# Turning scaled tiles by a product with a diagonal, and two moves in the order of a block's products

## The chip, the cores and the metric

The kernel runs on one core of one Trainium2 chip. The metric is the device time of one execution in microseconds (us), as the median of several runs. Engines are named as in the profile: PE (TensorE matmul) with PEld (its weight load), DVE (VectorE), ACT (ScalarE), POOL (GpSimd), SP (SyncE, whose queue issues the DMAs).

## The reference

One layer of a hybrid encoder block on 2048 tokens of width 1024, in float32:

```python
xn = rms_norm(x, ln_mix_g)
proj = xn @ w_in
y = concat(mlstm_group(proj...), mla_group(proj...))      # mLSTM in both directions, attention
h = x + y @ w_out                                         # "out" stage
h = h + conv_gated_mlp(rms_norm(h, ln_ffn_g))             # w_up, 3-tap conv, silu gate, w_down
gate = sigmoid(rms_norm(h, ple_norm_g) @ w_ple_gate)      # "gate" stage
h = h + gate * rms_norm(p @ w_ple_proj, ple_post_g)
return rms_norm(h, final_g)
```

`rms_norm(x, g)` is `x * rsqrt(mean(x*x) + 1e-6) * g` over the 1024 columns.

## The kernel before, in words

The tokens are cut into 16 tiles of 128 rows. After the input projection, the mLSTM and the attention, everything from `w_out` on runs in one loop, `Block.stream`, over "pairs" `i`: -8 to -1 is the out stage (two token tiles each), 0 to 43 the up projection of the MLP (two blocks of 22, one for each half of the tokens), 44 to 67 the down projection (three blocks of 8), 68 (`NG`) to 75 the gate stage. A run of pairs that shares its large operand is a block, so the block changes at i = 0, 22, 44, 52, 60 and 68.

Each pair computes a 2x2 block product by Strassen's method in Winograd's form, with seven products. `prod(out, w, x)` (line 1435) issues one of them: 128x128 pieces of the pair's own operand as weights against 512 columns of the block's operand. Both are split into a high and a low part (fp32r), and three of the four combinations are multiplied, 12 matmuls for four k pieces, 9 where the block has three. The order in program text is A11 B11 (into PSUM tile x, "fx" in the trace), S1 T1 (z, "fz"), A22 T4 of the pair before (`rest_y(prev)`, into its y, weights "fwd"), S2 T2 (y, "fy"), A12 B21 (x), S4 B22 of the pair before (`rest_z(prev)`, z), S3 T3 (y). A22 T4 accumulates in the same bank y that S3 T3 left, so the addition on DVE that reads S3 T3 (line 1420, into uv, xt or fh) comes before it.

The block's operands B11, T1, T2, B21, T3, T4 and B22 come by DMA as raw tiles ("opr", a few places in rotation), and `load_op` splits them: a cast on ACT (line 120, or 128 with a gain), then a subtraction on DVE (line 123, or 129 with a gain), into "op". `load(then, name)` does this for the next block, in the last pair of the block before. A raw tile's place is loaded anew (`op_fill`) once it is split. `up_prep` prepares the pair's own operand for the next pair ("fw", "fwd"), with the same casts and subtractions.

In the out stage, `Out.done` stores a finished tile t to h1_d by DMA and squares it on ACT with row sums; POOL makes the inverse norm r, a column of one value for each token. `Out.scaled` (line 1706) then multiplies the 128x1024 tile by r in place on ACT, and `Out.turn` turns it, four 128x128 transpositions (line 1716, with the identity `b.ident` as moving operand) into one PSUM bank, which ACT copies out (line 1718, or 1721 with a gain for i < -4) for the store to x2_d. `Out.beside` places these steps beside the products of later pairs: `scaled` at sides 7 and 1, the four turns of a pair's two tiles at sides 1 to 4 two pairs later.

In the gate stage the pair's own operand is made from tiles of h2_d: `load_tile` loads them ("ha"), `Gate.turn` transposes them (line 1842) at sides 1, 2, 4 and 5 of the pair before they are used. In the first gate pair, i = `NG`, side 1 turns tile 2. Its place, w7, held the first output tile of pair NG-2 until that was complete and stored by `rest_z` (line 1463).

The order on each engine is not that of the text. A planner orders the instructions of each engine from their order in the text and its own estimates of when their inputs are there. `keep_in_program_order(ins)` pins an instruction behind the one that stands before it in the text on the same engine.

Of the kernel before, what the change touches and what calls it, by code (L numbers as in the profile page):

```python
# [13 lines left out]
AF = mybir.ActivationFunctionType  # L14
ALU = mybir.AluOpType
# [4 lines left out]
P = 128  # L20
# [15 lines left out]
SB = 512  # L36
# [24 lines left out]
class Block:  # L61
# [51 lines left out]
        t = self.smp.tile([P, 1 if n == 1 else 8], F32, name=name, tag="c1" if n == 1 else "c8")  # L113
        return t[:, 0:n]

    def split(self, src, hi, lo, act=True, sub=None):

        nc = self.nc
        if act:
            nc.scalar.copy(hi, src)  # L120
        else:
            nc.vector.tensor_copy(hi, src)
        (sub or nc.vector).tensor_tensor(lo, src, _f(hi), op=ALU.subtract)  # L123

    def split_g(self, src, g, hi, lo):

        nc = self.nc
        nc.scalar.activation(hi, src, AF.Copy, scale=g)
        nc.vector.scalar_tensor_tensor(lo, src, g, _f(hi), op0=ALU.mult, op1=ALU.subtract)

    def mm3(self, out, lh, ll, rh, rl, first, last, more=False):

# [1141 lines left out]

    def load_op(self, blk, n):

        self.xop[n] = [self.early.get((blk, n, k)) or self.split_op() for k in range(self.BLOCKS[blk][2])]

    def split_soon(self, n):

# [1 line left out]
            item = self.loaded[0][0]  # L1282
            self.early[item] = self.split_op()

    def split_op(self):

        (blk, n, k), raw, _ = self.loaded.pop(0)
        hi, lo = self.op_place(blk, n, k)
        gain = {2: self.g2, 6: self.g3}.get(blk)
        if gain is not None and n[0] == "B":  # L1290
            kt = k + (int(n[1]) - 1) * 4
            self.split_g(raw, gain[0][:, kt:kt + 1], hi, lo)
        else:
            self.split(raw, hi, lo)
        self.op_fill()
        return hi, lo

# [118 lines left out]
    def stream(self, out):  # L1416

        nc = self.nc
# [5 lines left out]
        first = self.o  # L1424
# [1 line left out]
        class Pair:  # L1426
            pass

        def prod(out, w, x, more=False, cols=slice(0, SB)):
            wh, wl = w  # L1430
            ops = self.xop[x]
            first, last = not more, len(ops) - 1
            for a, lo in ((wh, 0), (wl, 0), (wh, 1)):
                for k, parts in enumerate(ops):
                    nc.tensor.matmul(out, a[:, k * P:(k + 1) * P], parts[lo][:, cols], start=first,  # L1435
                                     stop=lo == 1 and k == last, skip_group_check=more)
                    first = False

        def rest_y(s):

            prod(s.y, s.ops["A22"], "T4", True)
            if s.acc:
                add(s.o[1][:, L], s.o[1][:, L], s.y)
                if s.out:
                    first.done(s, 1)
                    return
                nc.sync.dma_start(self.h2_d[2 * s.pr + 1], s.o[1])
                if s.i >= gate.first - 8:
                    gate.factor(s.o[1], 2 * s.pr + 1)
            elif s.gate:  # L1450
                gate.part(s, 1, 0, s.y)
            else:
                nc.scalar.copy(s.uv[:, 2:2 + SB], s.y)

        def rest_z(s):

            prod(s.z, s.ops["S4"], "B22", True)
            if s.acc:
                add(s.o[0][:, H], s.o[0][:, H], s.z)
                if s.out:  # L1460
                    first.done(s, 0)
                    return
                nc.sync.dma_start(self.h2_d[2 * s.pr], s.o[0])
                if s.i >= gate.first - 8:
                    gate.factor(s.o[0], 2 * s.pr)
            elif s.gate:
                add(s.c12, s.c12, s.z)
                gate.part(s, 0, 1, s.c12)
            else:
                add(s.ug[:, 2 + SB:2 + 2 * SB], s.ug[:, 2 + SB:2 + 2 * SB], s.z)  # L1470
# [42 lines left out]
        prev, n = None, blocks[-1][0] + blocks[-1][1]  # L1513
# [7 lines left out]
        NG = NUP + 24  # L1521
        for i in range(blocks[0][0], n):
            blk = max(q for q, bl in enumerate(blocks) if bl[0] <= i)
            j = i - blocks[blk][0]
            then = blk + 1 if j == blocks[blk][1] - 1 and blk + 1 < len(blocks) else None

            def load(b, name):
                if b is not None:
                    self.load_op(b, name)

            def side(at):

                bank = prev.spare if at % 2 and prev else s.spare
                first.beside(s, at, bank)
                gate.beside(s, at, bank)

            s = Pair()
# [6 lines left out]


            prod(x, s.ops["A11"], "B11")
            nc.scalar.copy(s.y, x)  # L1547
            if s.acc:
                s.o = first.tiles if s.out else outs.pop(i)
            load(then, "B11")  # L1550
            side(1)
            prod(s.z, s.ops["S1"], "T1")
            if not s.acc:
                s.p5 = self.at("t4" if s.gate else f"t{6 + i % 2}", [P, SB], name="p5")
                nc.scalar.copy(s.p5, s.z)
            load(then, "T1")
            side(2)
            if prev:
                rest_y(prev)
                if prev.up:  # L1560
                    conv(prev, 1)
            if i == n - 1:
                rest_z(prev)
            if j == 0 and blk:
                load(blk, "T4")
            side(3)
            prod(s.y, s.ops["S2"], "T2", True)
            if s.acc:
                add(s.o[0][:, H], s.o[0][:, H], s.y)
            elif s.gate:  # L1570
# [12 lines left out]
                self.up_prep(i + 1)  # L1583
            if 0 <= i < NG - 2:
                self.up_load(i + 2)
            prod(x, s.ops["A12"], "B21", True)
            if s.acc:
                add(s.o[0][:, L], s.o[0][:, L], x)
            elif s.gate:
# [4 lines left out]
            if NG <= i + 1 < n:  # L1594
                self.up_prep(i + 1)
            if prev and i < n - 1:
                rest_z(prev)
                if prev.up:
                    conv(prev, 0)
            if j == 0 and blk:  # L1600
# [3 lines left out]
            if NUP < i < NG - 1:  # L1604
                outs[i + 1] = self.down_out(i + 1)
            side(6)
            load(then, "B21")
            prod(s.y, s.ops["S3"], "T3", True)
            if i == NUP:
                c22 = self.at("t7", [P, SB], name="c22")  # L1610
                nc.scalar.copy(c22, s.y)
                add(c22, c22, s.z)
                s.o += self.down_out(NUP, (1,))
                add(s.o[1][:, H], s.o[1][:, H], c22)
                outs[i + 1] = self.down_out(i + 1)
            elif s.acc:
                add(s.o[1][:, H], s.o[1][:, H], s.y)
                add(s.o[1][:, H], s.o[1][:, H], s.z)
            elif s.gate:
                add(s.p5, s.p5, s.y)  # L1620
                gate.part(s, 1, 1, s.p5)
            else:
                s.uv = self.at("u2", [P, 2 * SB + 2], name="uv")
                add(s.uv[:, 2 + SB:2 + 2 * SB], s.p5, s.y)
                if i in steps:
                    self.p1tag = f"t{6 + i % 2}"
                    next(steps[i])
            load(then, "T3")
            side(7)
            if i < NG - 2 and any(bl[0] + bl[1] - 2 == i for bl in blocks[:-1]):  # L1630
                self.op_begin(blk + 1)
            prev = s
# [21 lines left out]
class Out:  # L1654
# [3 lines left out]
    def __init__(self, b):  # L1658
        self.b, self.nc, self.d = b, b.nc, b.d
        self.rot, self.tiles, self.next, self.norm = _rot("", ("w11", "u2", "u0", "u1", "w7")), None, [], {}  # L1660
        self.parts = {}

    def tile(self, i, e):

# [38 lines left out]

    def scaled(self, i, e):
        t, r = self.norm[i, e]
        self.nc.scalar.activation(t, t, AF.Copy, scale=r)

    def turn(self, i, e, f, bank):

        b, nc = self.b, self.nc  # L1710
        t, c = self.norm[i, e][0], self.tile(i, e)
        xo = b.at(f"t{4 + f if i > -5 else 2 * e + f}", [P, 4, P], name="nt_o")
        pt = bank.rearrange("p (k t) -> p k t", t=P)
        for j in range(4):
            kt = f * 4 + j
            nc.tensor.transpose(pt[:, j], t[:, kt * P:(kt + 1) * P], b.ident)
        if i > -5:
            nc.scalar.copy(xo, pt)
        else:
            for j in range(4):  # L1720
                nc.scalar.activation(xo[:, j], pt[:, j], AF.Copy, scale=b.g2[0][:, f * 4 + j:f * 4 + j + 1])
            self.parts[f, e] = xo
        nc.sync.dma_start(b.x2_d[:, f * 4:f * 4 + 4, c * P:(c + 1) * P], xo)
# [321 lines left out]
```

## Time and profile before

| | |
|---|---|
| median of 3 runs | 2899.16 us (2894.27 to 2899.87) |
| profiled execution | 2900.96 us, of which the span of the trace is 2899.2 |
| PE busy | 2853.5 us, 98% of the span |
| DVE, ACT, POOL busy | 2041.1, 1524.4, 158.0 us |
| DMA | 508.94 MB, mean 176 GB/s |
| out stage, in the trace | from about 1232 us; its last turn at 1435 us |
| change from block 1 to block 2 | about 1806 to 1840 us |
| first gate pair | begins at 2717.40 us |

A row of a group in the profile gives line, engine, operation, output and inputs, count, then busy us, mean ns of one, and the idle time of the engine before them with what ended it. A row of the timeline gives start, duration (of a merged run of instructions), engine, line, names, shape, count, and in brackets the idle time before it and its releaser. Matmuls are pipelined: the duration of one is longer than the distance to the next one's start.

### The profile page before, as it was taken

Reading aid. Unit: us, or ns where it says so; the run is one execution under the profiler, and the core shown is the slowest. Engines: PE = TensorE matmul, PEld = TensorE weight load, DVE = VectorE, ACT = ScalarE, POOL = GpSimd, SP = SyncE. Lnnn points to the kernel's source line nnn. Section 1 sums busy time; section 2 is a strip of 40 time slices with the busy share of each in tenths; the row PEclk is TensorE's granted clock in tenths of the full one; section 3 lists DMA queues with packets and bytes.
Section 4 is the critical chain, followed back from the end, with each engine's and each line's share of the span. In section 5 each row is a group of like instructions: output and inputs, shape, how many; then the busy total and the mean of one; then the engine's idle time right before and its main releaser. Section 6 shows DMA issues by size and latency. Waiting matters only on the chain.

```text
span 2899.2 us, 40167 instructions
## 1 busy us (share of the span) xinstructions
PE 2853.5 (98%) x14110; PEld 2390.1 (82%) x14110; DVE 2041.1 (70%) x3790; ACT 1524.4 (53%) x3014; POOL 158.0 (5%) x295
## 2 busy tenths in 40 slices
PE   8999999999999999999999999999999999999998
PEld 7888888888888888788788888788888788888787
DVE  7521555777777777876677877767777867576787
ACT  7311544556666566765755555655555423254765
POOL 3100000000000010001000000000000000002111
PEclk9999999999999999999999999999999999999999
DMA  6612545653333333478834554657776757476865
GB/s 194 127 59 76 162 122 165 218 160 118 107 111 97 97 116 110 129 240 266 266 139 170 188 178 141 212 179 232 231 240 207 243 176 263 158 260 213 274 214 163
DMA packets 408314, 508.94 MB, mean 176 GB/s; under 512 B 34080, under 2 KB 271664, under 8 KB 408112
## 3 DMA queue, kind: packets, MB, share of 16 engines
q1 hardware_dynamic: 408112, 506.37, 55.3%
q8 instruction: 111, 1.82, 0.3%
q14 instruction: 91, 0.75, 0.1%
HBM read 324.16 MB, written 182.12 MB: 175 GB/s over the span
## 4 chain that ended last, share of the span: by engine, by line
PE 84%; DMA 5%; DVE 5%; ACT 3%; issue 3%; POOL 1%; SPq 0%; ACTq 0%; POOLq 0%; DVEq 0%
PE fy L1435 21%; PE fz L1435 14%; PE fx L1435 14%; PE bk L133 13%; PE ppv L989 3%; PE tb L977 3%; PE bk L914 2%; PE bk L916 2%; PE bk L915 2%; PE bk L918 2%; PE bk L917 2%; PE fs L133 2%; PE ppv L990 2%; PE gb L133 1%; PE mb L852 1%
## 5 line engine op out<-in xcount | busy, mean ns | idle before, releaser
L1435 PE MATMUL fz<-op,fw 128*128 128x512 f32 x1968 | 477.1, 391 | 2.7 <-ACT fw L120 2.7
L1435 PE MATMUL fy<-op,fw 128*128 128x512 f32 x1968 | 478.1, 391 | 1.6 <-ACT fy L1547 1.6
L1435 PE MATMUL fx<-op,fw 128*128 128x512 f32 x1968 | 476.0, 390 | 0.0
L1435 PEld LDWEIGHTS fy<-op,fw 128*128 128x128 f32 x1968 | 370.4, 189 | 79.4 <-ACT fy L1547 2.4
L1435 PEld LDWEIGHTS fz<-op,fw 128*128 128x128 f32 x1968 | 367.5, 188 | 79.5 <-ACT fw L120 3.6
L1435 PEld LDWEIGHTS fx<-op,fw 128*128 128x128 f32 x1968 | 368.0, 188 | 76.2 <-ACT fy L1547 0.2
L1435 PE MATMUL fy<-op,fwd 128*128 128x512 f32 (+1 forms) x984 | 239.8, 392 | 2.8 <-DVE uv L1420 2.6
L120 ACT CAST pt<-tb 128x512 fp32r<-128x512 f32 x256 | 147.2, 587 | 171.2 <-PE tb L977 170.4
L133 PE MATMUL bk<-wsp,xh 128*128 128x512 f32 (+1 forms) x768 | 234.1, 386 | 0.0
L1435 PEld LDWEIGHTS fy<-op,fwd 128*128 128x128 f32 x984 | 183.7, 189 | 41.7 <-DVE uv L1420 3.7
L919 DVE TENSOR_REDUCE mx<-bk 128x1 f32<-128x512 f32 x256 | 174.7, 684 | 40.5 <-PE bk L918 39.3
L123 DVE TENSOR_TENSOR pt<-tb,pt 128x512 fp32r<-128x512 f32 x256 | 174.1, 684 | 30.7 <-ACT pt L120 28.9
L937 ACT ACTIVATE pe<-bk,nm 128x512 f32<-128x512 f32 x256 | 174.8, 696 | 38.2 <-DVE nm L931 33.5
L989 PE MATMUL ppv<-pt,kv 128*128 128x512 f32 x512 | 188.6, 406 | 0.5 <-DVE pt L123 0.5
L133 PEld LDWEIGHTS bk<-wsp,xh 128*128 128x128 f32 x768 | 145.2, 189 | 25.1
L133 PE MATMUL bk<-wsp,xl 128*128 128x512 f32 (+1 forms) x384 | 150.7, 392 | 7.7 <-DVE xl L123 7.7
L133 PE MATMUL bk<-xh,wqk 128*128 128x512 f32 x480 | 157.1, 393 | 0.0
L977 PE MATMUL tb<-ident,pe 128*128 128x128 f32 x1024 | 150.3, 273 | 4.4 <-DVE pt L123 3.8
L990 PE MATMUL ppv<-pt,kv 128*128 128x256 f32 x512 | 144.7, 283 | 0.0
L977 PEld LDWEIGHTS tb<-ident,pe 128*128 128x128 f32 x1024 | 121.8, 140 | 25.0 <-DVE pt L123 6.8
L120 ACT CAST fw<-hraw 128x1024 fp32r<-128x1024 f32 (+1 forms) x72 | 70.2, 980 | 116.4 <-PE fx L1435 58.9
L123 DVE TENSOR_TENSOR fw<-fwr,fw 128x1024 fp32r<-128x1024 f32 x88 | 107.4, 1220 | 26.9 <-ACT fw L120 26.9
(363 smaller groups left out, 5113.5 us busy)
## 6 DMA issues: line engine op xcount, KB each, us to landing
fwr<-in_w_up SPq DMA_DIRECT2D x66, 512.0 KB, 5.2
fh<-h_d SPq DMA_DIRECT2D x48, 512.0 KB, 4.2
h_d<-fh SPq DMA_DIRECT2D x48, 512.0 KB, 4.0
s_d<-fwr SPq DMA_DIRECT2D x44, 512.0 KB, 3.3
fws<-s_d SPq DMA_DIRECT2D x44, 512.0 KB, 3.7
rw<-row_d SPq DMA_DIRECT2D x32, 512.0 KB, 5.5
tw_d<-tsum SPq DMA_DIRECT2D x60, 256.0 KB, 5.4
opr<-tw_d SPq DMA_DIRECT2D x60, 256.0 KB, 4.7
```

What stands on the lines that cost most here:

```text
L120: nc.scalar.copy(hi, src)
L123: (sub or nc.vector).tensor_tensor(lo, src, _f(hi), op=ALU.subtract)
L133: mm = lambda *a, **k: self.nc.tensor.matmul(*a, **k, skip_group_check=more)
L914: mm(ps, ql, kh[:, ks], start=True, stop=False)
L915: mm(ps, qr, self.krl[:, ks], start=False, stop=False)
L916: mm(ps, qh, kl[:, ks], start=False, stop=False)
L919: nc.vector.tensor_reduce(s.mx[:, kb:kb + 1], ps, axis=AX.X, op=ALU.max)
L937: nc.scalar.activation(s.pe[:, kb % 2], s.banks[kb], AF.Exp, bias=s.nm, scale=ASCALE, accum_out=s.rs[:, kb:kb + 1])
L977: nc.tensor.transpose(t[:, j, :], s.p[kb][:, j * P:(j + 1) * P], self.ident)
L989: mm(w.ps, vh[:, ks], pts[kb][:, j], start=kt == 0, stop=False, skip_group_check=True)
L990: mm(w.ps[:, 0], vl[:, ks], pts[kb][:, j, 0], start=False, stop=kt == NT - 1, skip_group_check=True)
L1435: nc.tensor.matmul(out, a[:, k * P:(k + 1) * P], parts[lo][:, cols], start=first, stop=lo == 1 and k == last, skip_group_check=more)
```

## The change

Three edits.

1. `Out.scaled` no longer scales the tile. It writes a 128x128 tile "diag", the identity times r, in a place of its own (s0 or s1), and `Out.turn` replaces each transposition by an ordinary f32 product of the tile's 128x128 piece with that diagonal.
2. `load(then, "B21")` moves from ahead of S3 T3 to behind S3 T3's addition, ahead of `load(then, "T3")`; the DVE halves of these splits are pinned in the order of the text.
3. At i = NG, `rest_y(prev)` (A22 T4 of the last down pair) moves from behind side 2 to between side 1 and S1 T1. The first matmul of each of A22 T4, S1 T1, S2 T2, A12 B21 and S4 B22 of the pair before is pinned there in the order of the text.

```diff
-    def split(self, src, hi, lo, act=True, sub=None):
+    def split(self, src, hi, lo, act=True, sub=None, pin=False):
...
-        (sub or nc.vector).tensor_tensor(lo, src, _f(hi), op=ALU.subtract)
+        a = (sub or nc.vector).tensor_tensor(lo, src, _f(hi), op=ALU.subtract)
+        if pin:
+            self.tc.keep_in_program_order(a)
...
-        self.xop[n] = [self.early.get((blk, n, k)) or self.split_op() for k in range(self.BLOCKS[blk][2])]
+        self.xop[n] = [self.early.get((blk, n, k)) or self.split_op(n == "B21") for k in range(self.BLOCKS[blk][2])]
...
-                    nc.tensor.matmul(out, a[:, k * P:(k + 1) * P], parts[lo][:, cols], start=first,
-                                     stop=lo == 1 and k == last, skip_group_check=more)
-                    first = False
+                    m = nc.tensor.matmul(out, a[:, k * P:(k + 1) * P], parts[lo][:, cols], start=first,
+                                         stop=lo == 1 and k == last, skip_group_check=more)
+                    if pin:
+                        self.tc.keep_in_program_order(m)
+                    first = pin = False
...
             load(then, "B11")
             side(1)
-            prod(s.z, s.ops["S1"], "T1")
+            if i == NG:
+                rest_y(prev, True)
+            prod(s.z, s.ops["S1"], "T1", pin=i == NG)
...
             side(2)
-            if prev:
+            if prev and i != NG:
                 rest_y(prev)
...
-            prod(s.y, s.ops["S2"], "T2", True)
+            prod(s.y, s.ops["S2"], "T2", True, pin=i == NG)
...
-            prod(x, s.ops["A12"], "B21", True)
+            prod(x, s.ops["A12"], "B21", True, pin=i == NG)
...
-                rest_z(prev)
+                rest_z(prev, i == NG)
...
             side(6)
-            load(then, "B21")
             prod(s.y, s.ops["S3"], "T3", True)
...
+            load(then, "B21")
             load(then, "T3")
...
     def scaled(self, i, e):
         t, r = self.norm[i, e]
-        self.nc.scalar.activation(t, t, AF.Copy, scale=r)
+        dg = self.diag[i, e] = self.b.at(f"s{e}", [P, P], name="diag")
+        self.nc.scalar.activation(dg, self.b.ident, AF.Copy, scale=r)
...
-            nc.tensor.transpose(pt[:, j], t[:, kt * P:(kt + 1) * P], b.ident)
+            nc.tensor.matmul(pt[:, j], t[:, kt * P:(kt + 1) * P], self.diag[i, e], start=True, stop=True)
```

More of the change, by code (lines that the diff above doesn't have):

```diff
@@ L122, in split, with split_g @@
             nc.vector.tensor_copy(hi, src)
-        (sub or nc.vector).tensor_tensor(lo, src, _f(hi), op=ALU.subtract)
-    def split_g(self, src, g, hi, lo):
+        a = (sub or nc.vector).tensor_tensor(lo, src, _f(hi), op=ALU.subtract)
+        if pin:
+            self.tc.keep_in_program_order(a)
+    def split_g(self, src, g, hi, lo, pin=False):
         nc = self.nc
         nc.scalar.activation(hi, src, AF.Copy, scale=g)
-        nc.vector.scalar_tensor_tensor(lo, src, g, _f(hi), op0=ALU.mult, op1=ALU.subtract)
+        a = nc.vector.scalar_tensor_tensor(lo, src, g, _f(hi), op0=ALU.mult, op1=ALU.subtract)
+        if pin:
+            self.tc.keep_in_program_order(a)
     def mm3(self, out, lh, ll, rh, rl, first, last, more=False):
@@ L1283, in split_soon, with split_op @@
             self.early[item] = self.split_op()
-    def split_op(self):
+    def split_op(self, pin=False):
         (blk, n, k), raw, _ = self.loaded.pop(0)
@@ L1291, in split_op @@
             kt = k + (int(n[1]) - 1) * 4
-            self.split_g(raw, gain[0][:, kt:kt + 1], hi, lo)
+            self.split_g(raw, gain[0][:, kt:kt + 1], hi, lo, pin)
         else:
-            self.split(raw, hi, lo)
+            self.split(raw, hi, lo, pin=pin)
         self.op_fill()
@@ L1427, in stream, with prod @@
             pass
-        def prod(out, w, x, more=False, cols=slice(0, SB)):
+        def prod(out, w, x, more=False, cols=slice(0, SB), pin=False):
             wh, wl = w
@@ L1434, in prod, with rest_y @@
                 for k, parts in enumerate(ops):
-                    nc.tensor.matmul(out, a[:, k * P:(k + 1) * P], parts[lo][:, cols], start=first,
-                                     stop=lo == 1 and k == last, skip_group_check=more)
-                    first = False
-        def rest_y(s):
-            prod(s.y, s.ops["A22"], "T4", True)
+                    m = nc.tensor.matmul(out, a[:, k * P:(k + 1) * P], parts[lo][:, cols], start=first,
+                                         stop=lo == 1 and k == last, skip_group_check=more)
+                    if pin:
+                        self.tc.keep_in_program_order(m)
+                    first = pin = False
+        def rest_y(s, pin=False):
+            prod(s.y, s.ops["A22"], "T4", True, pin=pin)
             if s.acc:
@@ L1453, in rest_y, with rest_z @@
                 nc.scalar.copy(s.uv[:, 2:2 + SB], s.y)
-        def rest_z(s):
-            prod(s.z, s.ops["S4"], "B22", True)
+        def rest_z(s, pin=False):
+            prod(s.z, s.ops["S4"], "B22", True, pin=pin)
             if s.acc:
@@ L1660, in __init__ @@
         self.rot, self.tiles, self.next, self.norm = _rot("", ("w11", "u2", "u0", "u1", "w7")), None, [], {}
-        self.parts = {}
+        self.parts, self.diag = {}, {}
     def tile(self, i, e):
```

## The prediction

> **What bounds the kernel now.** I read the page's first part, then who PE waited for from 1236 us to the end (out stage to gate stage), then the stretches, then the timeline around each wait that is left.
>
> ```profile
> PE 2853.5 (98%) x14110; PEld 2390.1 (82%) x14110; DVE 2041.1 (70%) x3790; ACT 1524.4 (53%) x3014; POOL 158.0 (5%) x295
> ```
> ```profile
> PE fz L1435 <- ACT fw L120: 2.7, 2, 1.8
> PE fs L1716 <- ACT nt_o L1718: 2.7, 1, 2.7
> PE fy L1435 <- DVE uv L1420: 2.6, 2, 1.8
> PE fs L1716 <- ACT xt L1706: 2.0, 1, 2.0
> PE fy L1435 <- ACT fy L1547: 1.6, 1, 1.6
> PE fs L1842 <- DMA ha<-h_d: 0.9, 1, 0.9
> PE fy L1435 <- DVE xt L1420: 0.2, 1, 0.2
> ```
> ```profile
> 1250.00:1380.00 130.00, 130.00 (x619) 107.39 (x618) 86.04 (x118) 75.19 (x160) 15.88 (x36) 1.00 0.79 251
> 1380.00:1390.00 10.00, 7.30 (x31) 5.74 (x30) 6.94 (x12) 8.97 (x17) 0.00 (x0) 0.83 0.52 149
> ```
>
> The columns of the waits are total us, times, longest; those of a stretch its length, then PE, PEld, DVE, ACT and POOL busy, granted clock, DMA share and GB/s. PE is the bound. In 1663 us it waits 12.7 us, in nine places. From 1250 to 1380 us, the heart of the out stage, it has no gap at all: whatever a changed instruction adds to PE there is added to the end, and relief of ACT or DVE is worth only the waits in that list and the slower products behind them (granted clock 0.83 where a gap of 2.7 us falls).
>
> **The turns: what they cost on PE.** The change makes each transposition of line 1716 a plain f32 product with a scaled diagonal. A plain f32 product of 128x128 by 128 columns exists in this kernel: line 838, the mLSTM scores, called 4 times in each of 16 chunks.
>
> ```profile
> L838 PE MATMUL mb<-qk 128*128 128x128 f32 x128 | 17.2, 275 | 0.0
> ...
> L1716 PE MATMUL fs<-ident,xt 128*128 128x128 f32 x128 | 19.7, 278 | 4.7 <-ACT nt_o L1718 2.7 <-ACT xt L1706 2.0
> ```
> ```profile
> 735.66 1.05 PE L838 MATMUL mb<-qk 128*128 128x128 f32 x8
> 736.47 0.47 PE L914 MATMUL bk<-kv,q_s 128*128 128x512 f32 x1
> ...
> 1342.60 0.60 PE L1716 MATMUL fs<-ident,xt 128*128 128x128 f32 x4
> 1342.96 2.99 PE L1435 MATMUL fx<-op,fw 128*128 128x512 f32 x12
> ```
>
> Line 838 has 64 calls and 128 records, line 1716 has 128 calls (16 tiles of 8) and 128 records: a plain f32 product runs as two, a transposition as one. In time it is the same two to one: four products are eight records and hold PE from 735.66 to 736.47, 0.81 us; four transpositions from 1342.60 to 1342.96, 0.36 us. So a group of four grows by 0.45 us, and there are 32 groups (16 tiles, two halves): **+14.4 us**. No gap can hide it before 1380 us. The ends are 0, if the second record slipped under the stream of large products, and three times more, 1.08 us a group, if the array needed four of what a transposition needs. I take 0.45, since line 838's eight stand in just such a stream of 512-column products. By the Trainium skill ("TensorE: Matmul & The Clock Gate", Terms) its transpose mode is four times faster for FP32, and "FP8 and Floating Point Precision" (TensorE Precision Notes) gives true FP32 four passes; by these the term would be about +35 us, an estimate, and the trace of line 838 speaks for half of that ratio.
>
> **The turns: what they free on ACT.**
>
> ```profile
> L1706 ACT ACTIVATE xt<-xt,rsr 128x1024 f32<-128x1024 f32 x16 | 18.5, 1153 | 25.1 <-DMA h_d<-xt 23.4 <-issue 0.8 <-POOL rsr L143 0.8
> ```
> ```profile
> L862 ACT ACTIVATE hy<-mb,den 128x128 f32<-128x128 f32 x64 | 20.3, 371 | 12.0 <-DVE den L858 10.6 <-PE bk L917 1.4
> ```
> ```profile
> 1379.85 1.15 ACT L1706 ACTIVATE xt<-xt,rsr 128x1024 f32<-128x1024 f32 x1 [5.77 <-DMA h_d<-xt]
> ...
> 1428.98 1.15 ACT L1706 ACTIVATE xt<-xt,rsr 128x1024 f32<-128x1024 f32 x1 [0.69 <-DMA h_d<-xt]
> ```
> ```profile
> 1384.12 1.11 PE L1716 MATMUL fs<-ident,xt 128*128 128x128 f32 x4 [2.70 <-ACT nt_o L1718]
> 1384.89 4.11 PE L1435 MATMUL fy<-op,fw 128*128 128x512 f32 x12
> ...
> 1430.18 0.66 PE L1716 MATMUL fs<-ident,xt 128*128 128x128 f32 x4 [1.95 <-ACT xt L1706]
> 1430.59 4.58 PE L1435 MATMUL fy<-op,fw 128*128 128x512 f32 x12
> ```
>
> Line 1706 scales the tile in place, so it must wait until the store to h1_d has read it: 23.4 us of ACT standing still, with casts and copies queued behind. The new instruction writes 128x128 into a place of its own; line 862, a copy with a column's scale of that size, takes 0.371 us against 1.153. ACT gets 16 x 0.78 = 12.5 us and the 23.4 us of waiting back, but the path gets only two stalls. At 1384.12 the copy out of PSUM that PE waits for stood behind the 5.77 us wait: 2.70 us of gap, 0.51 in the slow turn (1.11 against 0.60), 1.12 in the product after it (4.11 against 2.99), 4.3 us, and all of it should go. At 1430.18 it is 1.95 + 0.06 + 1.59 = 3.6 us; the store's wait (0.69) and the shorter instruction (0.78) explain 1.5 of the 1.95, so between 1.5 and 3.6 goes; I take 3.0, nearer the upper end, because an ACT lighter by all of the above also reaches this place sooner. Together **-7.3 us** (-5.8 to -7.9). The new wait, of the products for the diagonal, stands on ACT where the tile's scaling stood, 0.78 us shorter, so it is no later.
>
> **B21 behind S3 T3's addition.** It acts at the six changes of block. At the change to block 2 the splits of B21 (line 129, the DVE half) stand ahead of the addition that frees fy for A22 T4:
>
> ```profile
> 1826.56 0.74 DVE L129 SCALAR_TENSOR_TENSOR op<-opr,gt,op 128x512 fp32r<-128x512 f32 x1
> ...
> 1828.42 0.74 DVE L129 SCALAR_TENSOR_TENSOR op<-opr,gt,op 128x512 fp32r<-128x512 f32 x1
> ...
> 1830.28 1.40 DVE L129 SCALAR_TENSOR_TENSOR op<-opr,gt,op 128x512 fp32r<-128x512 f32 x2
> ...
> 1832.74 0.67 DVE L1420 TENSOR_TENSOR uv<-p,fy 128x512 f32<-128x512 f32 x1
> ```
> ```profile
> 1833.47 4.61 PE L1435 MATMUL fy<-op,fwd 128*128 128x512 f32 x12 [1.80 <-DVE uv L1420]
> ```
>
> Four splits are 0.74 + 0.74 + 1.40 = 2.9 us; without them the addition comes at about 1829.9 and the wait of 1.80 us is gone, with the slow product after it (4.61 against 2.99: 1.62): 3.4 us. The other wait on uv (2.6 - 1.8 = 0.8) and the one on xt (0.2) are of the same kind. Sum **-4.4 us**; the other changes of block show no wait and gain nothing. What may be late next is the loads: a raw tile comes free only when it is split, so T3's loads start up to 2.9 us later; T3 is used three products of nearly 3 us after A22 T4, about 8 us, which I take as cover enough. Without it the cost is up to those 2.9 us a change of block.
>
> **A22 T4 ahead of S1 T1 at the gate.** Here PE waits 1.77 us for the split of S1 (the longest of the first row of the waits). The change puts the nine products of A22 T4 there, and pins their first one behind everything PE has been given so far. But the last of that is the turn that `side(1)` issues, of tile 2 of h2, and before the change this turn ran much later:
>
> ```profile
> 2713.20 2.32 PE L1435 MATMUL fz<-op,fw 128*128 128x512 f32 x9
> ...
> 2717.40 2.88 PE L1435 MATMUL fx<-op,fw 128*128 128x512 f32 x12
> 2722.05 1.21 PE L1435 MATMUL fz<-op,fw 128*128 128x512 f32 x4 [1.77 <-ACT fw L120]
> ...
> 2725.45 1.98 PE L1435 MATMUL fy<-op,fwd 128*128 128x512 f32 x8
> 2727.27 0.60 PE L1842 MATMUL fs<-ident,ha 128*128 128x128 f32 x4
> ```
> ```profile
> 2727.20 0.43 PEld L1842 LDWEIGHTS fs<-ident,ha 128*128 128x128 f32 x4 [0.19 <-DMA ha<-h_d]
> ```
> ```profile
> 2719.02 0.32 SPq L1463 DMA_DIRECT2D h_d<-fh  x1
> ...
> 2722.75 0.80 SPq L1826 DMA_DIRECT2D ha<-h_d  x2
> ```
> ```profile
> 2718.32 0.68 DVE L1420 TENSOR_TENSOR fh<-fh,fz 128x512 f32<-128x512 f32 x1
> ```
>
> The turn's weights waited for the load of ha and started as it landed, at 2727.2. That load goes into the place (w7) of an output tile that is complete with the addition at 2718.32, is stored at 2719.02 and frees its place at 2722.75. So the turn cannot come much before 2727, and A22 T4, S1 T1 and all behind them on PE now stand behind it. The 5.2 us of products that PE did from 2722.05 to 2727.27 move behind the turn. The addition comes up to 0.7 us sooner, as one B21 split no longer stands ahead of it, and a gap of some 6 us leaves slow products behind, 1.6 us as after the gaps above: 5.2 - 0.7 + 1.6 = **+6.1 us**. Ends: if the addition followed the product's end (2713.20 + 2.32) at once, 2.8 us sooner, and no slow product came, +2.4; if the clock stayed low for twice as long, +7.7. Below nothing only if the turn is early after all (a rival).
>
> **Sum.** 14.4 - 7.3 - 4.4 + 6.1 = +8.8 us. The profiled execution took 2900.96 us (span 2899.2 and 1.76 around it), so it would take 2909.8; the median of the runs is 1.8 lower, 2899.16, and the forecast for it is **2908 us**, 0.3% slower. Its own range, with each term between its ends, is 2903 to 2914.
>
> **The rivals.**
> - *The turn at the gate is early enough.* Then the gate's edit does what it says: the wait of 1.77 us goes, +6.1 becomes -1.8, and the sum is +0.9: 2900. Against it speaks the row of the weight load that waits for ha; for it, that the order of SP and DVE ahead of the gate is planned anew.
> - *The plain turn costs PE no more than the transposition* (the other side): the second record slips under the neighbours, the first term is 0, and the sum is -5.6: 2893.5; it decides from a group of under about 0.4 us. Against it: line 838's eight records take as long as eight transpositions would (0.81 is over twice 0.36).
> - *The plain turn takes four times the transposition*: 32 x 1.08 = 34.6 instead of 14.4, sum +29: 2928. The Trainium skill's pages named above would have it so; line 838 speaks against it.
> - *B21 too late*: its splits and the loads behind them now miss their products, the 4.4 us are not gained and one wait of up to 2.9 us comes: +16.1: 2915. For it: DVE is full at these places; against: 8 us of cover.
>
> **How the numbers follow.** A measurement of this kernel can tell about 0.2% (5.8 us) from no change: the limits are 2893.4 and 2905.0. Forecast 0.56, of which 0.46 lies above 2905.0 and 0.10 within; early turn 0.17 (0.13 within, 0.04 below); free turn 0.10 (0.06 below, 0.04 within); fourfold turn 0.05 and late B21 0.12, both above. Faster 0.10, same 0.27, slower 0.63. The range, 2897 to 2917, holds the forecast's own, the early turn and the late B21; outside stay the free and the fourfold turn and a little of the tails.
>
> **What would show it.** Right: line 1716's successor with 256 records and 0.8 us from its first to the next product; the stalls at 1384, 1430 and 1833 gone; no wait of ACT on h_d; PE idle some 6 us behind A11 B11 of the first gate pair, ended by ha. Wrong: turn groups still near 0.36 us, a gate gap under 2 us, or new waits on B21 or T3 casts at a change of block.

## The result and the profile after

| | before | after |
|---|---|---|
| median of 5 runs | 2897.71 us (2894.27 to 2899.87) | 2916.77 us (2914.35 to 2918.88) |
| profiled execution, span | 2899.2 us | 2915.8 us |

The changed kernel is slower: ratio 1.0062, 95% interval 1.0051 to 1.0073. The forecast was 2908.0 us with a range of 2897 to 2917, so the direction was right and the size was not: +19.1 us where +8.8 was expected. The median lies 0.2 us inside the range, two of the five runs lie beyond it, and the forecast's own range, 2903 to 2914, does not hold it: that the number falls inside is luck, and the wide range reached so far only for the rival of the late B21 (2915).

First the busy row of the page of after, then who PE waited for from 1236 us to the end (total us, times, longest).

```profile
PE 2868.2 (98%) x14238; PEld 2407.1 (83%) x14238; DVE 2043.8 (70%) x3790; ACT 1513.9 (52%) x3014; POOL 158.5 (5%) x295
```
```profile
PE fs L1851 <- DMA ha<-h_d: 5.6, 2, 3.6
PE fy L1439 <- DVE fh L1424: 3.4, 2, 2.4
PE fz L1439 <- ACT fw L120: 2.0, 1, 2.0
PE fy L1439 <- DVE uv L1424: 1.9, 1, 1.9
PE fy L1439 <- ACT fy L1553: 1.3, 1, 1.3
PE fz L1439 <- DVE fw L123: 0.4, 1, 0.4
```

PE is busy 14.7 us longer. No turn of an output tile waits any more (the old waits on nt_o and xt are gone), but fh, the output tiles of the down blocks, is new in the list with 3.4 us, uv has kept 1.9, and ha has grown from 0.9 to 5.6 us.

The groups of the turns and of the new instruction on ACT (busy us, mean ns), the timeline where the stalls of 1384 and 1430 us were, and a stretch of the whole out stage, of after and then of before (length, then PE, PEld, DVE, ACT, POOL busy, granted clock, DMA share, GB/s):

```profile
L1725 PE MATMUL fs<-diag,xt 128*128 128x128 f32 x256 | 33.7, 274 | 0.0
...
L1715 ACT ACTIVATE diag<-ident,rsr 128x128 f32<-128x128 f32 x16 | 6.5, 403 | 18.0 <-POOL rsr L147 18.0
```
```profile
1383.25 1.05 PE L1725 MATMUL fs<-diag,xt 128*128 128x128 f32 x8
1384.06 3.00 PE L1439 MATMUL fz<-op,fw 128*128 128x512 f32 x12
...
1428.76 1.05 PE L1725 MATMUL fs<-diag,xt 128*128 128x128 f32 x8
1429.57 2.98 PE L1439 MATMUL fz<-op,fw 128*128 128x512 f32 x12
```
```profile
1236.00:1450.00 214.00, 212.70 (x1065) 179.62 (x1064) 148.26 (x207) 123.36 (x260) 24.94 (x48) 1.00 0.80 254
```
```profile
1236.00:1450.00 214.00, 207.56 (x962) 170.21 (x961) 148.87 (x210) 136.10 (x264) 22.00 (x48) 0.98 0.81 257
```

256 records, 0.81 us from the first of a group to the next product (1383.25 to 1384.06), no gap and no slow product, so the stalls of 1384 and 1430 us are gone. Over the out stage PE goes from 207.56 to 212.70 us of 214, ACT from 136.10 to 123.36.

At the change to block 2 the addition on uv is indeed early (1830.90), and A22 T4 starts without a wait. One pair later the same wait is back, with the slow product behind it. The timeline of after, DVE and PE:

```profile
1830.90 0.68 DVE L1424 TENSOR_TENSOR uv<-p,fy 128x512 f32<-128x512 f32 x1
...
1856.68 0.68 DVE L1424 TENSOR_TENSOR uv<-p,fy 128x512 f32<-128x512 f32 x1
1857.41 4.61 PE L1439 MATMUL fy<-op,fwd 128*128 128x512 f32 x12 [1.91 <-DVE uv L1424]
```

Two later changes of block have waits that before had not, at pairs 44 and 60:

```profile
2263.93 0.62 ACT L120 CAST op<-opr 128x512 fp32r<-128x512 f32 x1 [2.22 <-DMA opr<-tw_d]
...
2271.65 0.68 DVE L1424 TENSOR_TENSOR fh<-fh,fy 128x512 f32<-128x512 f32 x1
...
2272.39 3.06 PE L1439 MATMUL fy<-op,fw 128*128 128x512 f32 x12 [2.36 <-DVE fh L1424]
...
2572.60 0.62 ACT L120 CAST op<-opr 128x512 fp32r<-128x512 f32 x1 [3.19 <-DMA opr<-tw_d]
...
2583.75 2.33 PE L1439 MATMUL fy<-op,fwd 128*128 128x512 f32 x9 [1.00 <-DVE fh L1424]
```

And the gate, where PE idles 3.62 us behind A11 B11 until ha has landed:

```profile
2727.88 0.69 DVE L1424 TENSOR_TENSOR fh<-fh,fz 128x512 f32<-128x512 f32 x1 [0.55 <-PE fz L1439]
...
2729.72 2.88 PE L1439 MATMUL fx<-op,fw 128*128 128x512 f32 x12
...
2732.17 0.79 SPq L1835 DMA_DIRECT2D ha<-h_d  x2
...
2736.23 1.09 PE L1851 MATMUL fs<-ident,ha 128*128 128x128 f32 x4 [3.62 <-DMA ha<-h_d]
2736.97 4.19 PE L1439 MATMUL fy<-op,fwd 128*128 128x512 f32 x9
```

To see where time is lost, the start of one instruction of every pair (ACT's copy of A11 B11 from fx to fy) is compared between two traces. This table, worked out from the timelines, gives how much later it comes than in the profiled execution of before, in us, by pair. The kernels below "after" are those of the experiments.

| kernel | -8 | 3 | 21 | 24 | 43 | 47 | 59 | 63 | 66 | 69 | 75 |
|---|---|---|---|---|---|---|---|---|---|---|---|
| after | -0.1 | 5.1 | 5.1 | 4.8 | 4.8 | 7.3 | 7.3 | 9.7 | 9.7 | 16.5 | 16.5 |
| turns alone | 2.9 | 9.7 | 9.7 | 7.9 | 7.9 | 7.1 | 7.1 | 7.1 | 7.1 | 9.5 | 9.4 |
| B21 alone | 1.5 | 1.0 | 1.1 | 1.1 | 1.1 | 3.2 | 3.2 | 4.8 | 4.8 | 7.4 | 7.1 |
| gate alone | 2.6 | 1.0 | 1.0 | -1.0 | -1.0 | -0.3 | -0.3 | -0.3 | -0.3 | 7.4 | 7.4 |
| gate, A22 T4 ahead of the turn | 1.4 | 1.1 | 1.1 | -1.1 | -1.1 | -2.2 | -2.2 | -2.2 | -2.2 | -0.7 | -0.2 |
| B21 and B22 | 2.6 | 3.1 | 3.2 | -0.9 | -0.9 | 1.7 | 1.7 | 3.8 | 3.8 | 4.5 | 5.0 |
| B21, T4 behind | -1.4 | -4.2 | -4.2 | -5.8 | -5.8 | -4.2 | -4.2 | -2.6 | -2.6 | -1.1 | -1.6 |
| scaling on POOL | 0.0 | -4.2 | -4.2 | -5.6 | -5.6 | -6.2 | -6.2 | -6.2 | -6.2 | -5.1 | -5.2 |
| all moves, scaling on POOL | -2.1 | -4.4 | -4.4 | -8.5 | -8.5 | -7.1 | -7.1 | -5.2 | -5.1 | -2.6 | -3.1 |
| block 2 only | 0.8 | -1.3 | -1.3 | -5.4 | -5.4 | -6.3 | -6.3 | -6.4 | -6.3 | -3.6 | -3.7 |
| block 2 only, scaling on POOL | -2.5 | -7.9 | -7.9 | -12.0 | -12.0 | -11.6 | -11.6 | -11.6 | -11.6 | -9.8 | -10.0 |

Each row is one execution, and unchanged code scatters. From pair -8 to 3 the kernels with the old out stage move by -2.9 to +0.5, from 21 to 24 those with the old order there by -2.2 to -1.4, from 43 to 47 by -1.1 to +0.8, from 66 to 69 those with the old gate and no B21 move by +1.1 to +2.7. Before's own execution was the unlucky one at 21 to 24 and a lucky one at the gate. From 59 to 63 nothing scatters. The verdicts below go by the medians; the table only tells where.

### The profile page after: what moved, and what is told of

Same layout as the page of the kernel before. It is cut to its first block, busy times and chain, and to the rows that moved or that the text cites. A ratio compares the mean times of both kernels' runs of the same rounds, so it can differ in the third digit from the quotient of the medians.

```text
span 2915.8 us, 40418 instructions
## 1 busy us (share of the span) xinstructions
PE 2868.2 (98%) x14238; PEld 2407.1 (83%) x14238; DVE 2043.8 (70%) x3790; ACT 1513.9 (52%) x3014; POOL 158.5 (5%) x295
## 5 line engine op out<-in xcount | busy, mean ns | idle before, releaser
L120 ACT CAST op<-opr 128x512 fp32r<-128x512 f32 x165 | 97.0, 621 | 64.0 <-DMA opr<-tw_d 25.4
```

## The experiments

The medians of before that stand beside them were 2899.15 us (first four kernels), 2899.79 (next four) and 2899.48 (last two); each ratio is taken from all the runs beside them and can differ from the quotient of the two medians by some 0.0006 (1.7 us). The differences in us below are those of the medians.

**The three parts alone.** First the turns: only the products with the diagonal.

```diff
-        self.nc.scalar.activation(t, t, AF.Copy, scale=r)
+        dg = self.diag[i, e] = self.b.at(f"s{e}", [P, P], name="diag")
+        self.nc.scalar.activation(dg, self.b.ident, AF.Copy, scale=r)
...
-            nc.tensor.transpose(pt[:, j], t[:, kt * P:(kt + 1) * P], b.ident)
+            nc.tensor.matmul(pt[:, j], t[:, kt * P:(kt + 1) * P], self.diag[i, e], start=True, stop=True)
```

> Only the diagonal products, the order of blocks and gate as before. Theory (32 turns lengthened by 0.45 us on a PE without gaps, less the stalls at 1384, 1404 and 1430 us that go): the pairs from i = 3 on run 5 us later than before, nothing is added after that, and the end comes 5 us later (ratio about 1.0017). Rival (the new instructions also shift the planned order further on, and the new waits at pairs 44, 60 and 67 of the whole change are theirs): 10 us or more.

Measured: 2906.76 us, ratio 1.0030 (1.0018 to 1.0042), +7.6 us. This lies between the two expectations. The table puts +6.8 of it in the out stage and shows no loss at 43 to 63, as the theory had it.

Then B21 alone: `load(then, "B21")` behind the S3 T3 addition at all six changes of block, with the pinned splits; turns and gate as before.

```diff
             side(6)
-            load(then, "B21")
             prod(s.y, s.ops["S3"], "T3", True)
...
+            load(then, "B21")
             load(then, "T3")
```

> Only B21 behind S3 T3's addition, transpositions and gate as before. Theory (the splits moved past the addition make the loads and splits of T3, T4 and B22 late, and the same stall comes one pair later): 4 us won at pair 22 and lost again at pair 23, some 2.5 us lost at pair 44 and at pair 60, 4 to 7 us slower in all (ratio about 1.002). Rival (the prediction's term): 4.4 us faster (0.9985).

Measured: 2904.92 us, ratio 1.0025 (1.0015 to 1.0036), +5.8 us: a loss, not a gain. It stays level at 21 to 24, where unchanged code gains 1.4 to 2.2 on this execution of before, and it loses 2.2 us at 43 to 47 and 1.6 at 59 to 63. The splits and the additions on uv and fh that DVE does at pair 44, in this kernel and then in the one with the gate alone, whose order there is the old one:

```profile
2251.03 0.68 DVE L1424 TENSOR_TENSOR uv<-p,fy 128x512 f32<-128x512 f32 x1
...
2253.96 1.29 DVE L123 TENSOR_TENSOR op<-opr,op 128x512 fp32r<-128x512 f32 x2
...
2256.31 2.49 DVE L123 TENSOR_TENSOR op<-opr,op 128x512 fp32r<-128x512 f32 x4
...
2260.64 0.69 DVE L123 TENSOR_TENSOR op<-opr,op 128x512 fp32r<-128x512 f32 x1 [0.63 <-ACT op L120]
...
2263.86 0.69 DVE L123 TENSOR_TENSOR op<-opr,op 128x512 fp32r<-128x512 f32 x1 [0.79 <-ACT op L120]
...
2265.67 2.49 DVE L123 TENSOR_TENSOR op<-opr,op 128x512 fp32r<-128x512 f32 x4
2268.07 0.69 DVE L1424 TENSOR_TENSOR fh<-fh,fy 128x512 f32<-128x512 f32 x1
```
```profile
2255.12 0.68 DVE L1424 TENSOR_TENSOR uv<-p,fy 128x512 f32<-128x512 f32 x1
2255.72 1.89 DVE L123 TENSOR_TENSOR op<-opr,op 128x512 fp32r<-128x512 f32 x3
...
2260.12 0.69 DVE L123 TENSOR_TENSOR op<-opr,op 128x512 fp32r<-128x512 f32 x1 [2.51 <-ACT op L120]
...
2260.80 0.68 DVE L1424 TENSOR_TENSOR fh<-fh,fy 128x512 f32<-128x512 f32 x1
```

Between the addition on uv, which was moved ahead, and the next one, on fh, stand four splits in the old order and twelve in the new one: B21's four, T3's four, and T4's four too, which the planner had put behind the fh addition before. PE then waits 2.51 us for that addition, and some of the splits ahead of it wait for casts that wait for loads. Late loads alone do not explain it: in the old order a cast there waits longer still for its load, 5.62 us at 2259.47, and no product waits for the addition.

Third the gate alone, with all its pins; turns and B21 as before.

```diff
             side(1)
-            prod(s.z, s.ops["S1"], "T1")
+            if i == NG:
+                rest_y(prev, True)
+            prod(s.z, s.ops["S1"], "T1", pin=i == NG)
...
-            if prev:
+            if prev and i != NG:
                 rest_y(prev)
```

> Only A22 T4 ahead of S1 T1 in the first gate pair, pinned behind the turn of tile 2; B21 and transpositions as before. Theory (PE stands until the load of tile 2 lands): a gap of 4 to 6 us ended by ha behind A11 B11 of pair 68, 4 to 7 us slower (ratio about 1.002), nothing before pair 68. Rival (the gap of the whole change there needs the moved B21 too): the wait of 1.8 us for the split of S1 goes and the kernel is 1 to 2 us faster.

Measured: 2908.06 us, ratio 1.0037 (1.0024 to 1.0049), +8.9 us, above the 4 to 7 expected. PE waits 8.5 us for ha, in two places, and 6.68 of them make the gap:

```profile
2718.06 2.88 PE L1439 MATMUL fx<-op,fw 128*128 128x512 f32 x12
2727.63 1.09 PE L1850 MATMUL fs<-ident,ha 128*128 128x128 f32 x4 [6.68 <-DMA ha<-h_d]
2728.37 3.88 PE L1439 MATMUL fy<-op,fwd 128*128 128x512 f32 x9
```
```profile
2718.79 0.69 DVE L1424 TENSOR_TENSOR fh<-fh,fz 128x512 f32<-128x512 f32 x1
```

The addition that completes the tile in w7 comes 0.7 us after A11 B11 began (2718.79 against 2718.06). In after it comes 1.8 us ahead of it (2727.88 against 2729.72): 2.6 us sooner as PE sees it, and the gap is 3.06 us shorter. The moved B21 explains the smaller part of this. With B21 alone the addition still comes 0.5 us after A11 B11 began (2722.99 against 2722.49), and in the next kernel, which moves B21 at the gate too, 0.3 ahead of it (2715.74 against 2716.07). The rest is that PE was late in the execution of after: at an earlier turn of the gate's first tiles it waited 1.95 us and two slow products followed, where the gate alone waited 1.80 and had none. The turn and the first of these products, in after and then in the gate alone:

```profile
2716.43 0.66 PE L1851 MATMUL fs<-ident,ha 128*128 128x128 f32 x4 [1.95 <-DMA ha<-h_d]
2716.84 3.46 PE L1439 MATMUL fy<-op,fwd 128*128 128x512 f32 x9
```
```profile
2706.36 0.66 PE L1850 MATMUL fs<-ident,ha 128*128 128x128 f32 x4 [1.80 <-DMA ha<-h_d]
2706.78 2.33 PE L1439 MATMUL fy<-op,fwd 128*128 128x512 f32 x9
```

The two slow products took 3.46 and 2.71 us for 2.33 and 2.21, so 1.6 of the 3.06 us had been lost ahead of the gap already. From pair 66 to 69 the table has 7.6 us for the gate alone and 6.9 for after, a difference of 0.7. The three parts add up to 7.6 + 5.8 + 8.9 = 22.3 us against 19.1 measured. Each of the three has an interval of 3 us or more to either side, so this difference does not show that the parts act on one another.

**The gate with A22 T4 ahead of the turn.** B21 behind the addition only at the change to the gate; at i = NG, A22 T4 goes ahead of side 1 too, and only its first matmul is pinned.

```diff
+            if i == NG:
+                rest_y(prev, True)
             side(1)
             prod(s.z, s.ops["S1"], "T1")
...
-            if prev:
+            if prev and i != NG:
                 rest_y(prev)
```

> A22 T4 ahead of the turn of tile 2 as well as of S1 T1, only its first matmul pinned, and B21 behind the addition only at the change to the gate block. If the turn's load is what held A22 T4, PE now goes from A11 B11 straight to A22 T4 and on to S1 T1 without the gap of 1.8 us: 1.5 to 2.5 us faster than before (ratio about 0.9993). Rival (A22 T4 itself waits, for the addition of S3 T3 that is late on DVE): a gap of 2 to 5 us ended by the addition, 1 to 4 us slower.

Measured: 2899.03 us, ratio 0.9999 (0.9990 to 1.0008). The expected gain of 1.5 to 2.5 us did not come, but the large gap is gone, as PE has A22 T4 and seven matmuls of S1 T1 to do before the turn:

```profile
2718.79 2.20 PE L1439 MATMUL fy<-op,fwd 128*128 128x512 f32 x9
2720.83 1.75 PE L1439 MATMUL fz<-op,fw 128*128 128x512 f32 x7
2723.77 0.66 PE L1853 MATMUL fs<-ident,ha 128*128 128x128 f32 x4 [1.19 <-DMA ha<-h_d]
```

So the turn ahead of A22 T4, with its pin, is what cost the gate alone most of its 9 us. This kernel also has fewer pins and moves B21 at the gate, which brings the addition about 1 us sooner (0.7 after against 0.3 ahead of the start of A11 B11); that is little against a gap of 6.68. Even in this order the edit gains nothing: the wait of 1.77 us on S1 is replaced by one of 1.19 on ha, and smaller ones follow.

**B21 and B22.** B21 as above, and in the up blocks B22's splits behind the S3 T3 addition too, also pinned at block 2.

```diff
-            if j == 0 and blk:
+            if j == 0 and blk and not s.up:
                 load(blk, "B22")
...
                 add(s.uv[:, 2 + SB:2 + 2 * SB], s.p5, s.y)
+                if j == 0 and blk:
+                    load(blk, "B22")
```

> The B21 move alone (2904.92 when it ran), and in the up blocks the splits of B22 behind the addition of S3 T3 too. Theory (the addition that frees fy is late only because splits stand ahead of it on DVE; moving B21's alone let B22's splits do the same one pair later): the wait of 2.14 us on uv and the slow product behind it, 1.7 us, go, so some 3.8 us less than with B21 alone, about 2901; no wait over 1 us on uv is left around 1850. Rival 1 (DVE is full there, so the work only moves the stall to the next place): a wait of about 2 us comes elsewhere within the next two pairs, time unchanged at 2905. Rival 2 (later loads are the cause): casts wait longer for opr and PE for op, unchanged or slower, 2905 to 2908.

Measured: 2905.92 us, ratio 1.0016 (1.0007 to 1.0025), so the time came out as the rivals had it. But the place came out as the theory had it: 4.1 us are gained from pair 21 to 24, of which unchanged code shows 1.4 to 2.2, so some 2 to 2.7 are the edit's, and no wait on uv is left. DVE one pair after the change:

```profile
1849.26 0.68 DVE L1424 TENSOR_TENSOR uv<-p,fy 128x512 f32<-128x512 f32 x1
1851.05 0.75 DVE L131 SCALAR_TENSOR_TENSOR op<-opr,gt,op 128x512 fp32r<-128x512 f32 x1
```

The splits of B22 stand behind the addition. What is gained here is lost at 43 to 47 (+2.6) and 59 to 63 (+2.1), as with B21 alone.

**B21, T4 behind.** B21 as above; in the down blocks `load(blk, "T4")` moves behind the addition of S2 T2 to the output tile, so that T4's four splits follow it.

```diff
-            if j == 0 and blk:
+            if j == 0 and blk and not s.down:
                 load(blk, "T4")
...
                 add(s.o[0][:, H], s.o[0][:, H], s.y)
+                if j == 0 and s.down:
+                    load(blk, "T4")
```

> The B21 move alone (2904.92 when it ran), and in the down blocks the splits of T4 behind the addition of S2 T2 to the output tile. Theory (with B21's splits held back, DVE's order put T4's four splits ahead of the addition that frees fy at pair 44, and these wait for ACT casts that wait for loads): the wait of 2.51 us on fh near 2268 goes, some 2.5 us less, about 2902.5; the addition stands behind 8 splits instead of 12. Rival 1 (the loads of T3 and T4 are late and PE would wait for them anyway): a wait on op or fh of 2 us stays, 2904 to 2905. Rival 2 (the fast product that PE does sooner meets the next wait, on fw at 2274, 1.48 us before): that wait grows by what the first one loses, 2904 to 2905.

Measured: 2906.95 us (2899.52 to 2910.85), ratio 1.0023 (1.0015 to 1.0032): no gain over B21 alone. The profiled execution was the shortest of its twelve, so its row of the table is not typical. In it the fh addition comes 12.8 us after the pair's start instead of 15.9 (2259.13 - 2246.29; 2268.07 - 2252.21), and PE, which is there sooner, still waits 1.74 us. The order explains part of the loss at pair 44; the rest, and why the median did not move, stays open.

**The scaling on POOL.** ACT is freed, but the turns stay transpositions: what ACT's relief is worth without the price of the products.

```diff
-        self.nc.scalar.activation(t, t, AF.Copy, scale=r)
+        self.nc.gpsimd.tensor_scalar(t, t, r, None, op0=ALU.mult)
```

> The kernel before, with the scaling of the output tile in place by its inverse norms done on POOL instead of ACT; the turns stay transpositions. It separates what ACT's relief is worth from what the plain products cost. Theory (ACT's wait for the store and the 1.15 us of scaling made the two stalls, 4.3 and 3.6 us with the slow products): 4 to 8 us less than before, 2891 to 2895, if POOL scales 128x1024 in under about 3 us. Rival 1 (POOL needs over 4 us for it): the turn waits for POOL, 2899 to 2905. Rival 2 (POOL's work slows DVE beside it): DVE's 128x1024 instructions grow and PE waits for fw, 2899 to 2903.

Measured: 2896.05 us, ratio 0.9991 (0.9983 to 1.0000), -3.7 us, a little less than the 4 to 8 expected. POOL takes 3.17 us for a tile (ACT 1.15), and three turns still wait for it, one of them 2.0 us:

```profile
L1706 POOL TENSOR_SCALAR xt<-xt,rsr 128x1024 f32<-128x1024 f32 x16 | 50.7, 3168 | 33.0 <-DMA h_d<-xt 26.2 <-DVE xt L1420 4.2 <-DVE nt_o L1730 1.9
```
```profile
PE fs L1716 <- POOL xt L1706: 3.0, 3, 2.0
```

With the 3.0 us that PE waits for POOL added, the relief is worth 6.7 us by this estimate, near the 7.3 of the prediction. Between this kernel and the turns alone lie 11.3 us (7.6 + 3.7); with those 3.0 that is 14.3, an estimate of the price of the plain products; the intervals of the two ratios leave both estimates some 3 us to either side.

**All moves, scaling on POOL.** The edits of the last three together on top of B21 alone, the gate as before.

```diff
-            if j == 0 and blk:
+            if j == 0 and blk and not s.down:
                 load(blk, "T4")
...
-            if j == 0 and blk:
+            if j == 0 and blk and not s.up:
                 load(blk, "B22")
...
-        self.nc.scalar.activation(t, t, AF.Copy, scale=r)
+        self.nc.gpsimd.tensor_scalar(t, t, r, None, op0=ALU.mult)
```

> The B21 move with both companions (B22 behind the S3 T3 addition in the up blocks, T4 behind the S2 T2 addition in the down blocks) and the scaling on POOL, gate as before. If all three theories hold the terms add: 2904.9 - 3.8 - 2.5 - 6 = about 2892.5, some 0.2% under the kernel before. If the order of DVE is not the cause: 2899 to 2901 from the scaling alone. If the scaling on POOL gains nothing: 2898 to 2899.

Measured: 2898.58 us, ratio 0.9998 (0.9989 to 1.0007), 6 us above the 2892.5 that the three theories add up to, and in the band of the third expectation (the scaling on POOL gains nothing). The table has 4.1 us gained at 21 to 24, 1.4 lost at 43 to 47 and 1.9 at 59 to 63, and from -8 to 3 a gain of 2.2, no more than unchanged code shows. The loss at 59 to 63 on DVE and PE:

```profile
2558.46 0.69 DVE L123 TENSOR_TENSOR op<-opr,op 128x512 fp32r<-128x512 f32 x1 [1.52 <-ACT op L120]
```
```profile
2568.96 2.32 PE L1439 MATMUL fy<-op,fwd 128*128 128x512 f32 x9 [1.01 <-DVE fh L1424]
```

**Block 2 only.** The kernel before, with B21's and B22's splits behind the S3 T3 addition where block 2 begins and nowhere else (both pinned; the other blocks keep the old places), and the same with the scaling on POOL.

```diff
                 add(s.uv[:, 2 + SB:2 + 2 * SB], s.p5, s.y)
+                if j == 0 and blk == 2:
+                    load(blk, "B22")
+            if then == 2:
+                load(then, "B21")
             load(then, "T3")
```

> The kernel before, with the splits of B21 and B22 behind the addition of S3 T3 at the change to block 2 only; every other block change, the turns and the gate as before. Theory (the losses of the B21 move lie at pairs 44, 60 and the gate, its gain at block 2 is real once B22 moves too): 2 to 4 us less than before, 2895 to 2897, no wait on uv over 0.5 us between 1820 and 1865, and the offsets to the kernel before stay flat from pair 24 to the end. Rival (DVE is full and what is saved at block 2 is given back, or later executions vary more than the gain): 2898 to 2900.

> The same edit at block 2 with the scaling of the output tiles done in place on POOL. If the two gains add: 3.7 + 2 to 4 = 5.7 to 7.7 us less than before, 2891 to 2893. If the gain at block 2 is given back: that of the scaling alone, 2895 to 2896.

Measured: 2897.37 us, ratio 0.9994 (0.9985 to 1.0003), and with POOL 2894.66 us, ratio 0.9980 (0.9972 to 0.9989). The first is 2.1 us under before, at the lower end of what was expected, and its interval does not rule out no change. The second beats both kernels: 4.8 us under before, and further under after; 5.7 to 7.7 was expected if the two gains add in full. PE's waits on DVE and on ACT's copy in the first of them are these, besides one of 0.2 us on a split ahead of a turn; none on uv is left:

```profile
PE fy L1439 <- ACT fy L1553: 0.7, 1, 0.7
PE fy L1439 <- DVE xt L1424: 0.2, 1, 0.2
```

Both gain 4.1 us from 21 to 24, some 2 to 2.7 more than unchanged code, and have nothing lost at 59 to 63. The same two moves made at every change of block stand at 1.0016, at block 2 alone at 0.9994: by these ratios the other changes of block cost about 6 us.

## Why the prediction was right and wrong

- **Price of the turns: right.** Predicted +14.4, from line 838: two records for a plain product, 0.81 us a group. Measured 0.81 us a group, 256 records, 33.7 us against 19.7, +14.0. The rival of a free second record and that of a fourfold turn both fell. By the Trainium skill ("TensorE: Matmul & The Clock Gate", Terms; "FP8 and Floating Point Precision", TensorE Precision Notes) the ratio would be four; this trace shows two.
- **ACT's relief: right.** Predicted -7.3, both stalls gone. Both are gone and ACT no longer waits for the store. The out stage as a whole grew 5.1 us in the trace of after and 6.8 with the turns alone, against 6.9 by the prediction's terms (14.4 - 7.3 - 0.2); unchanged code scatters by some 3 us there.
- **B21: the step that failed.** Predicted -4.4, measured +5.8 alone; in the trace of after -0.3 at block 2, +2.6 at pair 44, +2.3 at pair 60. Four things were wrong. The gain was read from one place alone: the next addition that PE needs, a pair later, stands behind B22's splits, and moving B21 only let PE reach that wait (shown by B21 and B22, and by block 2 only). The gain was also read from one execution: four other kernels with the old order there (turns, gate, gate with A22 T4 ahead, scaling on POOL) waited 1.25 to 1.35 us instead of 1.80, with no slow product behind, as in this row of the gate alone:

```profile
1834.04 3.03 PE L1439 MATMUL fy<-op,fwd 128*128 128x512 f32 x12 [1.35 <-DVE uv L1424]
```

  The other changes of block were put down at nothing, because they showed no wait; there the held-back splits and the new order of DVE made one. And "about 8 us, which I take as cover enough" looked at PE's use of T3, while splits that wait for their casts hold up the additions queued behind them on DVE. The rival "B21 too late", with a chance of 0.12, named the loss and its size (up to 2.9 us a change of block, 2915 in all, the nearest of the numbers to the result), though not its way through the additions. That at pair 60 it is the loads' lateness, rather than the order, is argued from the waits of the casts (3.19 us at 2572.60), not shown by an experiment.
- **The gate: right in mechanism.** The turn was pinned behind a load that could not be early. Predicted +6.1, ends +2.4 to +7.7; the trace of after has +6.9 from pair 66 to 69, where unchanged code has +1.1 to +2.7. The gap is 3.62 us and not some 6, as the addition came at once (the prediction's lower end); PE was late there for the most part because of slow products a pair earlier. The two products behind the gap took 4.19 and 3.22 us, some 2.3 more than the usual pace, for the 1.6 of the prediction. With the gate alone the gap was the expected one (6.68 us). The wait of 1.95 us at the earlier turn need not come from the change: there it is 0.88 us in before, and 1.75 and 2.15 in two kernels that leave this turn as it was (A22 T4 ahead of the turn, scaling on POOL).
- **The sum.** In the traces the change costs 16.6 us (2915.8 - 2899.2) against 8.8: out stage 5.1 for 6.9, B21 4.6 for -4.4, gate 6.9 for 6.1. Most of the miss is B21's 9 us. One execution of before is the measure here: by the scatter of unchanged code its block 2 was slow by 1.4 to 2.2 us and its gate fast by 1.1 to 2.7, so that B21 cost more than 4.6 us and the gate less than 6.9. The ends that the terms state add up to 2904 to 2911; the 2914 of the forecast's own range is not explained there.

## What to carry over

A stall in front of an accumulation is removed only if every later addition on the same queue is looked at: moving four splits behind one addition moved the wait to the next addition behind four others, and gained only when those moved as well. An edit that applies to all changes of block must be priced at all of them, above all where nothing waits now: here the moves of B21 and B22 gained at one and lost at two. A gap that shrinks is not yet a gain: the gate's went from 6.68 to 3.62 us, but over the pairs around it only 0.7 us was saved, as PE had lost time just ahead of it. So count from a fixed place ahead of a stall to one behind it. And a stall that is to be removed should be measured in several executions: the 1.80 us at block 2, with a slow product behind, was 1.25 to 1.35 without one in four others.

## What the runs showed of the hardware

- A slow product follows some gaps of PE and not others, and the length of the gap does not decide it. At the change to block 2, one pair on, twelve matmuls took 4.62 us after a gap of 2.14 us (B21 alone) and 3.04 after 2.22 at the same place (B21, T4 behind). At the earlier turn of the gate nine took 3.46 us after 1.95 (after), and 2.33 and 2.31 after 1.80 and 2.15 (gate alone, scaling on POOL). The granted clock was 0.83 in the ten microseconds around before's 1.80 (1830 to 1840) and after's 1.95 (2716 to 2726), and 1.00 around the 1.35 and 1.80 of the gate alone. By the Trainium skill ("TensorE: Matmul & The Clock Gate", Part 1) the clock is judged in free-running windows of about 3.4 us, so where a gap falls in its window would matter. That would fit the scatter, but no run here tests it, and gaps this far under a window already cost the clock here.
- POOL takes 3.17 us to scale a 128x1024 f32 tile by a column, ACT 1.15.
- One trace is a sample: kernels with the same out stage differ by up to 3 us across it, and the wait at 1833 us, 1.80 us in before, was 1.25 to 1.35 in four others of the same order.
